# Decode scores in three runs a half batch, and the next chunk's first gate products ahead of a chunk's down products

## The chip, the cores and the metric

The kernel runs on one core of one Trainium2 chip. The metric is the device time of one execution in microseconds (us), from the first to the last instruction with what the device does around them. The kernel before takes 1250.42 us, the median of three runs (1248.77 to 1251.25).

The engines that the text speaks of: TensorE (PE in the profile, with its weight loads as PEld), VectorE (DVE), ScalarE (ACT), GpSimd (POOL), and SyncE (SP), which only issues DMAs here. Each runs its own list of instructions in order and waits for the others by semaphores.

## The reference, cut to what matters

One layer of a hybrid decoder is computed for a prompt group (512 tokens) and a sample group (8 sequences of 4 tokens, each with 4096 past tokens in a paged cache), with shared weights:

```python
h = h + 0.5 * rmsnorm(swiglu(rmsnorm(h, norm_g[0]), wg[0], wu[0], wd[0]), norm_g[1])
m, c_kv, k_r, s_fin = mixer(rmsnorm(h, norm_g[2]), ...)
h = h + rmsnorm(m, norm_g[3])
h = h + 0.5 * rmsnorm(swiglu(rmsnorm(h, norm_g[4]), wg[1], wu[1], wd[1]), norm_g[5])

def swiglu(x, wg, wu, wd):
    return (jax.nn.silu(x @ wg) * (x @ wu)) @ wd
```

Inside the mixer, the sample group attends to its cache in latent form. For each of the 8 sequences, 16 queries (4 tokens by 4 heads) of 256 + 64 elements meet 4096 past rows:

```python
s = (einsum('bqhr,bsr->bhqs', ql, c_kv) + einsum('bqhd,bsd->bhqs', qr, k_rope)) * scale
p = softmax(s)
out = einsum('bhqs,bsr->bqhr', p, c_kv)
```

## The kernel before

All big products are made of three fp32r matmuls for each pair of operands: a value is split in a high part (`wh`, `uh`, `hh`) and a remainder (`wl`, `ul`, `hl`). `weight` (lines 230 to 251) loads a weight block into `wraw` by an SP DMA, casts it to `wh` on ACT (line 250) and makes `wl` on DVE (line 251). The tokens are handled in two parts, `a` (256 columns) and `b` (288).

The change lies in one stage. There the second feed-forward network runs for part `a`, and woven into it is the decode attention of the sample group.

**The feed-forward side** is the generator `ffn(..., fine=True)`, called `gb`. It goes over 22 blocks `f` of the hidden width, in four chunks of 6, 6, 5 and 5 blocks (`FCH`). For a block it computes a gate product (24 matmuls: 8 blocks of depth by 3) and an up product (24), both at line 277, then `silu(gate) * up`, which is split into `hha` and `hla`. At the end of a chunk come the down products of the chunk for 8 column blocks `d`: the first two together in `gemm_2` (line 288), the others in `gemm` (line 259). They need the `hha` and `hla` of all the chunk's blocks. With `fine`, a gate or up product yields after half of it, so that a step of `gb` is 12 matmuls, or one down product.

**The decode side** is the generator `decode`, called `ga`. A half batch `H[n]` is 2048 past rows of one sequence; there are 16. Its work is spread over several rounds `n` of five steps `st`:

- POOL gathers two blocks of latent rows (`craw`, 1 MB each, line 1352, into seven slots) and two of rotary rows (`rraw`, line 1359, two buffers).
- DVE transposes them in five turns (`turn`, line 1367; two transposes each) into `kh`, a ring of four buffers (`KHB = 4`). `JS` says which columns a turn takes: the rotary rows first. `rraw` is free once the first turn has read it, and `gather_r` fetches the next.
- PE makes the scores in five parts (`score(k)`, line 1379). A part is 16 fp32 matmuls on tiles of 64 by 32 of the array, which the trace shows as 32 records. All parts add into two PSUM tiles `s`, copied out after the last one by ACT and DVE (line 1385). `RUNS` says at which step which parts are issued: before, parts 0 to 2 at step 2 and parts 3 and 4 at step 4.
- One round later, at step 1 (`PEAK`), `peak` finds the maximum (`pm`, line 1391), takes the exponentials (line 1397), transposes them and copies them to `pbuf` (line 1403, 12 copies on ACT and 4 on DVE); at step 4, `value` multiplies with `craw` (line 1412, 32 records).

A loop calls `ga` 94 times and `gb` 100 times by turns. A scheduler then orders each engine's list by readiness and priority, within the dependences; what it made is read from the built program's list.

The names of the steps: **run** is a row of score matmuls with no other PE work between them. **round** is the five steps.

Of the kernel before, what the change touches and what calls it, by code (L numbers as in the profile page):

```python
# [14 lines left out]
ALU = mybir.AluOpType  # L15
AX = mybir.AxisListType

P = 128
D = 1024
KD = D // P  # L20
# [5 lines left out]
HS = (256, T - 256)  # L26
# [38 lines left out]
JS = ((8, 9), (0, 1), (2, 3), (4, 5), (6, 7))  # L65
KHB = 4
PEAK = 1
RUNS = {2: (0, 1, 2), 4: (3, 4)}
LEVELS = (32, 16, 8, 4, 2, 1)
CH = 64  # L70

# [39 lines left out]
def hybrid_step_kernel(  # L111
# [5 lines left out]
    nc = tc.nc  # L117
# [55 lines left out]
    def tmp(tag, n, bufs=2, pool=sb):  # L173
        return mk([P, HM], F32, tag, bufs, pool=pool)[:, :n]
# [57 lines left out]
    def weight(srcs, kt, staged=False, home=None):  # L232
        if home is None and staged:
            pool, sfx, bufs = st, "x", STAG
        elif wx and wcnt[0] % (NW + WX) >= NW:
            pool, sfx, bufs = wx[0], "", WX
        else:
            pool, sfx, bufs = sb, "", NW
        w = mk([P, 8, P], F32, "wraw", 5, pool=sb)
        if home is None:  # L240
            wh = mk([P, 8, P], F32R, "wh" + sfx, bufs, pool=pool)
            wl = mk([P, 8, P], F32R, "wl" + sfx, bufs, pool=pool)
            wcnt[0] += not staged
        else:
            wh, wl = home
        n = P // len(srcs)
        for i, s in enumerate(srcs):
            nc.sync.dma_start(w[:, :kt, i * n : (i + 1) * n], s)
        with tc.issue_after(behind[1].ins) if behind[1] is not None else nullcontext():
            nc.scalar.copy(wh[:, :kt], w[:, :kt])  # L250
        nc.vector.tensor_tensor(wl[:, :kt], w[:, :kt], f32(wh[:, :kt]), op=ALU.subtract)  # L251
        return wh, wl, kt
# [16 lines left out]
    def gemm_q(wt, act_, step=2):  # L269
        wh, wl, kt = wt  # L270
        acc = ps("acc", "acc")
        n = act_[0].shape[-1]
        for k in range(kt):
            if k and k % step == 0:
                yield
            for i, (a, b) in enumerate(((wh, act_[0]), (wh, act_[1]), (wl, act_[0]))):
                nc.tensor.matmul(acc[:, :n], a[:, k], b[:, k], start=k + i == 0, stop=k == kt - 1 and i == 2)  # L277
        return acc[:, :n]
# [14 lines left out]
    def wcols(w, k0, kt, c0):  # L293
        return w[c0 // P, :, k0 : k0 + kt]
# [29 lines left out]
    def ffn(i, n_post, xs, u, nxt=None, mid=None, late=None, fin=None, pre=(), fine=False):  # L324
        pool = cur[-1]
        yield
        r2 = {x: u[x][2] for x in xs}
        mT = {x: actslot("m", x) for x in xs}
        ends = []
        for c, (f0, nf) in enumerate(FCH[i]):  # L330
            hh = {x: mk([P, FCH[i][0][1], HS[x]], F32R, "hh" + "ab"[x], pool=pool) for x in xs}
            hl = {x: mk([P, FCH[i][0][1], HS[x]], F32R, "hl" + "ab"[x], pool=pool) for x in xs}
            for j in range(nf):
                f = f0 + j
                wg_ = (w0 or [weight([wcols(w_g[i], 0, KD, f * P)], KD)]).pop(0)
                ga, up = {}, {}
                for x in xs:
                    ga[x] = (yield from gemm_q(wg_, u[x], 4)) if fine else gemm(wg_, u[x])
                if fine:
                    yield  # L340
                if late and f == 0:
                    behind[0] = late()
                wu_ = (w0 or [weight([wcols(w_u[i], 0, KD, f * P)], KD)]).pop(0)
                for x in xs:
                    up[x] = (yield from gemm_q(wu_, u[x], 4)) if fine else gemm(wu_, u[x])
                behind[1] = behind[0] if f == 1 else None
                for x in xs:
                    s = tmp("sil", HS[x], 3, pool)
                    t = tmp("sit", HS[x], 2, pool)
                    nc.vector.tensor_tensor(s, ga[x], r2[x], op=ALU.mult)  # L350
                    sigmoid(t, s)
                    nc.vector.tensor_tensor(s, s, t, op=ALU.mult)
                    nc.vector.tensor_tensor(s, s, up[x], op=ALU.mult)
                    split(hh[x][:, j], hl[x][:, j], s)
                yield
            last = c == len(FCH[i]) - 1
            if fin and c == BEG:
                fin.begin(u[xs[0]][2])
            if last:
                sacc = {x: tmp("ssm" + "ab"[x], HS[x], 1, pool) for x in xs}  # L360
            groups = [(d,) for d in range(KD)] if not last or len(xs) == 1 else [(d,) for d in range(KD - STAG)] + [tuple(range(KD - STAG, KD))]
            for grp in groups:
                if fine and not last and grp[0] == 0:
                    accs = yield from gemm_2([weight([wcols(w_d[i], f0, nf, d * P)], nf) for d in (0, 1)], (hh[xs[0]], hl[xs[0]]))
                elif fine and not last and grp[0] == 1:
                    accs = accs[1:]
                else:
                    accs = None
                wts = None if accs else {d: pre.pop(0) if pre else weight([wcols(w_d[i], f0, nf, d * P)], nf, len(grp) > 1) for d in grp}
                for x in xs:  # L370
                    for d in grp:
                        acc = accs[0] if accs else gemm(wts[d], (hh[x], hl[x]))
                        if last and fin and d == KD - 1:
                            fin.sums(sacc[x])
                        if c == 0:
                            nc.scalar.copy(mT[x][:, d], acc)
                        else:
                            nc.vector.tensor_tensor(mT[x][:, d], mT[x][:, d], acc, op=ALU.add)
                        if last:
                            sq = scale_sq(sacc[x], mT[x], d, gq, n_post, bool(fin) and d == KD - 1)  # L380
                        if last and fin and LAG <= d:
                            fin.column(mT[x], d - LAG)
                    if last and grp is groups[-1] and fin:
                        with tc.issue_after(fin.scale(sq).ins):
                            for d in range(KD - LAG, KD):
                                fin.column(mT[x], d)
                        fin.end(mT[x])
                    elif last and grp is groups[-1]:
                        ends.append(post(x, mT[x], sacc[x], u[x][2], nxt))
                        next(ends[-1])  # L390
                if not accs or grp[0] == 0:
                    yield
        if mid:
            mid()
        for p in ends:
            for _ in p:
                pass
# [14 lines left out]
    w0 = []  # L412
# [875 lines left out]
    with scope("dec"):  # L1288
# [134 lines left out]
        def decode():  # L1423
            H = [Half(n) for n in range(NH2)]
            blocks = [h_ for h_ in H for _ in range(2)]
            ups = [(h_, st) for h_ in H for st in range(len(JS))]

            def gather(n=1):
                for h_ in blocks[:n]:
                    h_.gather()  # L1430
                del blocks[:n]

            def turn():
                if ups:
                    h_, st = ups.pop(0)
                    h_.turn(st)
                    if st == 0 and h_.n + 1 < NH2:
                        H[h_.n + 1].gather_r()

            for n in range(NH2 + 4):  # L1440

                def at(k):
                    return H[n - k] if 0 <= n - k < NH2 else None

                for st in range(len(JS)):
                    if at(2):
                        for k in RUNS.get(st, ()):
                            at(2).score(k)
                    if n < 3 and st == 0:
                        if n == 0:  # L1450
                            H[0].gather_r()
                        gather(2 + n // 2)
                    if st == PEAK and at(3):
                        at(3).peak()
                    if st == 1 and at(4) and at(4).i:
                        at(4).gathered()
                    if st == len(JS) - 1 and at(3):
                        for c in range(2):
                            at(3).value(at(4), c)
                            gather()  # L1460
                    if n > 1 or n == 1 and st >= 1:
                        if n != 2 or st >= 2:
                            turn()
                    yield

        def decode_end():
# [228 lines left out]
```

## Time and profile before

| what | us |
|---|---|
| median of three runs | 1250.42 |
| the profiled execution, its own time | 1257.12 |
| its span from first to last instruction | 1255.3 |
| PE busy in it | 1225.7 |
| DVE busy in it | 983.8 |
| ACT busy in it | 742.0 |
| first and last score matmul, from the span's start | 716.2 and 953.2 |

The granted TensorE clock is 0.995 over the span and 1.00 from 716 us to 980 us.

A row of the timeline is: start, duration, engine, line, operation, output and inputs, the tile of the array, the shape, the number of equal instructions merged, and in brackets the idle time before it with what ended it. Matmuls overlap, so the durations of merged rows count from the first start to the last modelled end; the pitch, from start to start, is what PE spends. A row of waits is: who waited, for whom, in total, how often, the longest. A row of windows has for PE, PEld, DVE, ACT and POOL the busy time and the instructions, then the clock, the DMA share and the GB/s.

### The profile page before, as it was taken

The page shows a single profiled execution, that of the slowest core. Times are in us where ns is not written, and L with a number is a line of the kernel's source. Part 1 is how long each engine was busy: PE and PEld are TensorE (multiplying, and loading weights), DVE is VectorE, ACT ScalarE, POOL GpSimd, SP SyncE. Part 2 cuts the span into 40 slices and gives each one's busy share as a digit, 9 for nine tenths or more (in the row PEclk, how much of TensorE's full clock was granted, in tenths as well). Part 3 has the DMA queues.
Part 4 walks back from the last instruction along what each step waited for, and adds up shares of the span by engine and source line. Part 5 has one row for each costly group of instructions (what it writes and reads, how often), then busy time and mean ns, then how long its engine had stood idle before and what let it go on. Part 6 is the DMA issues. An engine that isn't in the chain of part 4 may idle for free.

```text
span 1255.3 us, 30001 instructions
## 1 busy us (share of the span) xinstructions
PE 1225.7 (98%) x12366; PEld 1157.1 (92%) x12366; DVE 983.8 (78%) x1976; ACT 742.0 (59%) x1559; POOL 72.4 (6%) x80
## 2 busy tenths in 40 slices
PE   8999999999999999999999899999999999999997
PEld 7999999999999988988889889878888999999997
DVE  7897788878679887877876899989987878466665
ACT  7675545544466655446668656665656777554454
POOL 0000000000000000000000412222310000000000
PEclk9999999999999999999999899999999999999999
DMA  6232333322164122324223959778776635645551
GB/s 236 85 118 87 100 101 101 94 96 94 51 227 158 60 89 69 104 77 148 75 92 118 374 178 347 292 249 299 252 273 218 204 104 191 188 137 182 145 160 59
DMA packets 73113, 195.59 MB, mean 156 GB/s; under 512 B 12336, under 2 KB 27728, under 8 KB 68240
## 3 DMA queue, kind: packets, MB, share of 16 engines
q1 hardware_dynamic: 64512, 150.47, 37.0%
q0 software_dynamic: 7168, 41.95, 9.2%
q8 instruction: 97, 1.59, 0.5%
q10 hardware_dynamic: 1296, 1.26, 0.3%
q14 instruction: 40, 0.33, 0.1%
HBM read 183.97 MB, written 9.67 MB: 154 GB/s over the span
## 4 chain that ended last, share of the span: by engine, by line
PE 86%; ACT 6%; DVE 5%; issue 2%; DMA 1%; SPq 0%; DVEq 0%; ACTq 0%
PE acc L259 29%; PE acc L277 18%; PE dn L259 8%; PE Y L561 6%; PE X L561 4%; PE Z L561 4%; PE s L1379 3%; PE acc L717 3%; PE o L1412 2%; ACT wh L250 1%; DVE wl L251 1%; PE pa L938 1%; ACT pbuf L1403 1%; PE acc L288 1%; PE zx L826 1%
## 5 line engine op out<-in xcount | busy, mean ns | idle before, releaser
L250 ACT CAST wh<-wraw 128x1024 fp32r<-128x1024 f32 (+2 forms) x194 | 185.3, 959 | 169.3 <-PE acc L259 108.6
L251 DVE TENSOR_TENSOR wl<-wraw,wh 128x1024 fp32r<-128x1024 f32 (+2 forms) x194 | 214.3, 1107 | 68.6 <-ACT wh L250 67.5
L277 PE MATMUL acc<-uha,wh 128*128 128x256 f32 (+1 forms) x528 | 155.7, 296 | 0.8 <-ACT uha L207 0.8
L277 PE MATMUL acc<-uha,wl 128*128 128x256 f32 (+1 forms) x528 | 150.6, 286 | 0.5 <-DVE wl L251 0.4
L277 PE MATMUL acc<-ula,wh 128*128 128x256 f32 (+1 forms) x528 | 150.9, 286 | 0.0
L259 PE MATMUL acc<-uhb,wh 128*128 128x288 f32 (+1 forms) x432 | 128.0, 296 | 0.0
L259 PE MATMUL acc<-uhb,wl 128*128 128x288 f32 (+1 forms) x432 | 127.0, 295 | 0.9 <-DVE wl L251 0.7
L259 PE MATMUL acc<-ulb,wh 128*128 128x288 f32 (+1 forms) x432 | 127.5, 295 | 0.0
L277 PEld LDWEIGHTS acc<-uha,wh 128*128 128x128 f32 x528 | 99.6, 189 | 8.8 <-issue 7.3
L277 PEld LDWEIGHTS acc<-uha,wl 128*128 128x128 f32 x528 | 99.5, 189 | 2.4 <-DVE wl L251 1.4
L277 PEld LDWEIGHTS acc<-ula,wh 128*128 128x128 f32 x528 | 99.8, 189 | 1.5 <-issue 1.2
L259 PEld LDWEIGHTS acc<-uhb,wl 128*128 128x128 f32 x432 | 81.2, 188 | 1.5 <-DVE wl L251 1.5
L259 PEld LDWEIGHTS acc<-uhb,wh 128*128 128x128 f32 x432 | 81.0, 188 | 0.2 <-ACT uhb L170 0.2
L259 PEld LDWEIGHTS acc<-ulb,wh 128*128 128x128 f32 x432 | 81.1, 188 | 0.1
L259 PE MATMUL dn<-hh,dh 128*128 128x272 f32 x256 | 74.3, 290 | 0.0
L259 PE MATMUL dn<-hh,dl 128*128 128x272 f32 x256 | 73.8, 288 | 0.0
L259 PE MATMUL dn<-hl,dh 128*128 128x272 f32 x256 | 73.6, 287 | 0.0
L1379 PE MATMUL s<-kh,q 64*32 64x128 f32 x2560 | 53.5, 273 | 5.3 <-issue 5.3
L277 PE MATMUL acc<-uhb,wh 128*128 128x272 f32 x176 | 52.8, 300 | 0.0
L1379 PEld LDWEIGHTS s<-kh,q 64*32 64x32 f32 x2560 | 38.5, 105 | 15.4 <-issue 10.5
L259 PE MATMUL acc<-hlb,wh 128*128 128x288 f32 x176 | 52.1, 298 | 0.0
L259 PE MATMUL acc<-hhb,wh 128*128 128x288 f32 x176 | 51.8, 298 | 0.0
(632 smaller groups left out, 3899.0 us busy)
## 6 DMA issues: line engine op xcount, KB each, us to landing
wraw<-w_u SPq DMA_DIRECT2D x66, 512.0 KB
wraw<-w_g SPq DMA_DIRECT2D x65, 512.0 KB
wraw<-w_d SPq DMA_DIRECT2D x40, 384.0 KB
wraw<-w_in SPq DMA_DIRECT2D x24, 512.0 KB
wraw<-w_d SPq DMA_DIRECT2D x32, 320.0 KB
wraw<-w_d SPq DMA_DIRECT2D x16, 512.0 KB
wraw<-w_o SPq DMA_DIRECT2D x16, 512.0 KB
g_S<-state SPq DMA_DIRECT2D x4, 512.0 KB
```

The source lines that it names most:

```text
L250: nc.scalar.copy(wh[:, :kt], w[:, :kt])
L251: nc.vector.tensor_tensor(wl[:, :kt], w[:, :kt], f32(wh[:, :kt]), op=ALU.subtract)
L259: nc.tensor.matmul(out, a, b, start=n == 0, stop=n == last)
L277: nc.tensor.matmul(acc[:, :n], a[:, k], b[:, k], start=k + i == 0, stop=k == kt - 1 and i == 2)
L288: nc.tensor.matmul(acc, a[:, k], b[:, k], start=k + i == 0, stop=k == kt - 1 and i == 2)
L561: nc.tensor.matmul(bank, a[p][:, k], b[q][:, k], start=first and k + n == 0, stop=k == 3 and n == 2, skip_group_check=True)
L717: nc.tensor.matmul(accs[x, d], wts[d][p][:, k], hs[k // 2][q][:, k % 2, x], start=k + n == 0, stop=k == nf - 1 and n == 2)
L826: nc.tensor.matmul(z, w[a][:, k], U[1][b][:, k], start=k + n == 0, stop=k == KD - 1 and n == 2)
L938: nc.tensor.matmul(po[es, c].rearrange("p (n m) -> p n m", m=m), kx[:, cs], up(qx[:, cs], m), start=True, stop=True, skip_group_check=True)
L1379: nc.tensor.matmul(self.s[r][c * 32 : c * 32 + 32, :P], q[rs, j], kh, start=st + jj == 0, stop=st == len(JS) - 1 and jj == 1, skip_group_c ...
L1403: (nc.scalar.copy if g else nc.vector.tensor_copy)(self.p[g * 32 : g * 32 + 32, c // 2, c % 2 * 4 : c % 2 * 4 + 4, self.i * 16 : self.i * ...
L1412: nc.tensor.matmul(o[g : g + 32, :R], self.p[:, c, a], self.craw[c][:, a], start=i + c == 0 and a < 4, stop=i + c == 2 and a >= 4, skip_gr ...
```

## The change

`RUNS` now gives the parts in three runs: 0 and 1 at step 0, 2 and 3 at step 2, 4 at step 4. So the first parts come two steps earlier, and the transposes that feed them do too: the exception for round 2 is dropped, and all later turns of `kh` stand two steps ahead of their old place.

In `ffn`, the gate product of a block and the `silu` behind it are taken out into `gate` and `swish`. With `fine`, at the end of a chunk that isn't the last, the gate product of the next chunk's first block is issued ahead of the chunk's down products, and its `silu` right behind it.

```diff
-RUNS = {2: (0, 1, 2), 4: (3, 4)}
+RUNS = {0: (0, 1), 2: (2, 3), 4: (4,)}
...
+        def swish(x, z):
+            s = tmp("sil", HS[x], 3, pool)
+            t = tmp("sit", HS[x], 2, pool)
+            nc.vector.tensor_tensor(s, z, r2[x], op=ALU.mult)
+            sigmoid(t, s)
+            nc.vector.tensor_tensor(s, s, t, op=ALU.mult)
+            return s
+
+        def gate(f):
+            w = (w0 or [weight([wcols(w_g[i], 0, KD, f * P)], KD)]).pop(0)
+            z = {}
+            for x in xs:
+                z[x] = (yield from gemm_q(w, u[x], 4)) if fine else gemm(w, u[x])
+            if fine:
+                yield
+            if late and f == 0:
+                behind[0] = late()
+            return {x: swish(x, z[x]) for x in xs} if fine else z
+
+        ahead = None
...
-                wg_ = (w0 or [weight([wcols(w_g[i], 0, KD, f * P)], KD)]).pop(0)
-                ga, up = {}, {}
-                for x in xs:
-                    ga[x] = (yield from gemm_q(wg_, u[x], 4)) if fine else gemm(wg_, u[x])
...
+                up = {}
+                sg = ahead if ahead else (yield from gate(f))
+                ahead = None
...
-                    s = tmp("sil", HS[x], 3, pool)
-                    t = tmp("sit", HS[x], 2, pool)
-                    nc.vector.tensor_tensor(s, ga[x], r2[x], op=ALU.mult)
-                    sigmoid(t, s)
-                    nc.vector.tensor_tensor(s, s, t, op=ALU.mult)
+                    s = sg[x] if fine else swish(x, sg[x])
                     nc.vector.tensor_tensor(s, s, up[x], op=ALU.mult)
                     split(hh[x][:, j], hl[x][:, j], s)
                 yield
             last = c == len(FCH[i]) - 1
+            if fine and not last:
+                ahead = yield from gate(f0 + nf)
...
-                        if n != 2 or st >= 2:
-                            turn()
+                        turn()
```

Each engine has the same instructions as before, by kind and shape; only their order differs, from the start of the decode stage to its end. What follows shows the list where the prediction looks at it.

PE, in one round in the middle of the stage, before (`pm` is the maximum of one half batch, `s` the scores of the next, `o` first the copied products of a finished pair turned around, then the products with the gathered slots `uhb` and `ha`; "..." stands for the network's matmuls):

```order
L1391 MATMUL pm<-ident,mxh 128x128
L1420 MATMUL o<-q_8159,q_8787 128x32 x2
...
L1379 MATMUL s<-kh,q_8159 32x128 x48
...
L1379 MATMUL s<-kh,q_8159 32x128 x32
L1412 MATMUL o<-uhb,pbuf 32x256 x8
L1412 MATMUL o<-ha,pbuf 32x256 x8
```

and the same round now:

```order
L1393 MATMUL s<-kh,q_8159 32x128 x32
...
L1405 MATMUL pm<-ident,mxh 128x128
L1434 MATMUL o<-q_8159,q_8787 128x32 x2
...
L1393 MATMUL s<-kh,q_8159 32x128 x32
...
L1393 MATMUL s<-kh,q_8159 32x128 x16
L1426 MATMUL o<-uhb,pbuf 32x256 x8
L1426 MATMUL o<-ha,pbuf 32x256 x8
```

There is one run more in a round, the first stands ahead of `pm`, and after the products with the slots only 12 of the network's matmuls stand ahead of the next round's first run. Over the whole list there are 37 runs before and 52 now; the rounds of the first two half batches are cut into more pieces in both.

DVE in the same round, before, from the transpose of the exponentials on (`hb`, `mb`, `q`, `dx` are gathered slots, `hla` and `sil` belong to the network):

```order
L1399 STREAM_TRANSPOSE pt<-q_8159 128x256
L1403 COPY pbuf<-pt 32x4x16 x4
L1367 STREAM_TRANSPOSE kh<-hb 128x512
L1367 STREAM_TRANSPOSE kh<-mb 128x512
L1367 STREAM_TRANSPOSE kh<-rraw 128x512 x2
L171 TENSOR_TENSOR hla<-sil,hha 128x256
L1367 STREAM_TRANSPOSE kh<-q_8787 128x512
L1367 STREAM_TRANSPOSE kh<-dx 128x512
```

and now:

```order
L1381 STREAM_TRANSPOSE kh<-hb 128x512
L1381 STREAM_TRANSPOSE kh<-mb 128x512
L336 TENSOR_TENSOR sil<-sil,sit 128x256
L1381 STREAM_TRANSPOSE kh<-rraw 128x512
L1407 TENSOR_REDUCE q_8159<-pm 128x16
L1435 COPY q_8787<-o 128x4x16
L1410 SCALAR_TENSOR_TENSOR mq,mbd<-q_8159 128x16
L1381 STREAM_TRANSPOSE kh<-rraw 128x512
L1413 STREAM_TRANSPOSE pt<-q_8159 128x256
L365 TENSOR_TENSOR sil<-sil,acc 128x256
L1417 COPY pbuf<-pt 32x4x16 x4
```

The turn of the rotary rows stood behind the copies to `pbuf`; now it stands ahead of them, in this round around the maximum `pm`.

SP, at the end of the network's first chunk, before and then now (`w_g`, `w_u` and `w_d` are the weights of gate, up and down products):

```order
L248 DMA wraw<-w_u 128x1024
L248 DMA wraw<-w_d 128x768 x8
L248 DMA wraw<-w_g 128x1024
L248 DMA wraw<-w_u 128x1024
```

```order
L248 DMA wraw<-w_u 128x1024
L248 DMA wraw<-w_g 128x1024
L248 DMA wraw<-w_d 128x768 x8
L248 DMA wraw<-w_u 128x1024
```

One gate weight of 512 KB went ahead of eight down weights, at each of the three boundaries between chunks, and its products with it.

More of the change, by code (lines that the diff above doesn't have):

```diff
@@ L334, in ffn @@
                 f = f0 + j
-                wg_ = (w0 or [weight([wcols(w_g[i], 0, KD, f * P)], KD)]).pop(0)
-                ga, up = {}, {}
-                for x in xs:
-                    ga[x] = (yield from gemm_q(wg_, u[x], 4)) if fine else gemm(wg_, u[x])
[L339 to L342, printed above, removed]
+                up = {}
+                sg = ahead if ahead else (yield from gate(f))
+                ahead = None
                 wu_ = (w0 or [weight([wcols(w_u[i], 0, KD, f * P)], KD)]).pop(0)
```

## The prediction

> **What bounds the kernel now.** I read the page's head first, then the stage that changes by windows, then who waits there, then the timeline of single rounds.
>
> ```profile
> span 1255.3 us, 30001 instructions
> PE 1225.7 (98%) x12366; PEld 1157.1 (92%) x12366; DVE 983.8 (78%) x1976; ACT 742.0 (59%) x1559; POOL 72.4 (6%) x80
> ```
>
> PE is the bound over the whole span. The lists of the two kernels differ in the decode stage alone, so only what PE spends there can change. This is the row of the stretch in which the rounds are regular, thirteen half batches from 752.75 to 947.78 us:
>
> ```profile
> 752.75:947.78 195.03, 189.07 (x3499) 163.16 (x3498) 177.00 (x390) 118.58 (x314) 46.38 (x47) 1.00 0.80 283
> ```
>
> PE is busy for 189.07 of 195.03 us, but DVE for 177.00, with the same work after the change. However much PE gains there, the stretch can't fall below 177: DVE is a second bound 18 us away. The waits of PE and of its weight loads from 716 to 955 us:
>
> ```profile
> PE s L1379 <- issue: 5.3, 18, 0.4
> PE acc L288 <- ACT hha L170: 0.6, 1, 0.6
> PE acc L277 <- DVE wl L251: 0.4, 1, 0.4
> PE pm L1391 <- DVE mxh L1387: 0.4, 1, 0.4
> ```
>
> ```profile
> PEld s L1379 <- issue: 10.5, 20, 0.6
> ```
>
> PE hardly waits for another engine. What it does lose is inside the score runs, for "issue", which is nothing that the profile shows: 10.5 us by the weight loads, whose ends are short (PE's own row counts less, since the modelled ends of 0.27 us cover part of each gap). Here is the timeline of PE in one such run, then that of GpSimd around it and after:
>
> ```profile
> 802.53 0.89 PE L1379 MATMUL s<-kh,q 64*32 64x128 f32 x42
> 803.59 0.43 PE L1379 MATMUL s<-kh,q 64*32 64x128 f32 x4 [0.17 <-issue]
> 804.34 0.42 PE L1379 MATMUL s<-kh,q 64*32 64x128 f32 x4 [0.32 <-issue]
> 805.06 0.51 PE L1379 MATMUL s<-kh,q 64*32 64x128 f32 x14 [0.29 <-issue]
> 805.49 0.42 PE L1412 MATMUL o<-uhb,pbuf 128*32 128x256 f32 x4
> ```
>
> ```profile
> 802.30 0.95 POOL L1359 DMA_INDIRECT rraw<-pool_r,idx  x1 [7.28 <-DVE kh L1367]
> 803.55 0.95 POOL L1359 DMA_INDIRECT rraw<-pool_r,idx  x1 [0.30 <-issue]
> 806.87 1.37 POOL L1352 DMA_INDIRECT uhb<-pool_c,idx  x1 [2.36 <-PE o L1412]
> 808.54 0.94 POOL L1352 DMA_INDIRECT ha<-pool_c,idx  x1 [0.30 <-issue]
> 816.57 0.95 POOL L1359 DMA_INDIRECT rraw<-pool_r,idx  x1 [7.09 <-DVE kh L1367]
> ```
>
> And a run of as many records that loses nothing, with GpSimd ahead of it:
>
> ```profile
> 774.92 1.16 PE L1379 MATMUL s<-kh,q 64*32 64x128 f32 x64
> 776.01 0.42 PE L1412 MATMUL o<-mb,pbuf 128*32 128x256 f32 x4
> ```
>
> ```profile
> 772.28 0.95 POOL L1359 DMA_INDIRECT rraw<-pool_r,idx  x1 [7.12 <-DVE kh L1367]
> 773.53 0.95 POOL L1359 DMA_INDIRECT rraw<-pool_r,idx  x1 [0.30 <-issue]
> ```
>
> The first takes 2.96 us to the next work (805.49 - 802.53), the second 1.09: 1.87 us are lost. In the first, after 42 records PE gets four at a time, at 0.04, 0.79 and 1.51 us after the second gather's start; in the second, the gathers began 2.6 us earlier and nothing happens. My reading, which is a coincidence of times and no more: while GpSimd issues two gathers, until 1.5 us after the second begins, PE's supply of instructions thins, and only a dense run (64 records in 0.9 us, against a network matmul each 0.12 us) empties what it has in store.
>
> **The change part by part.**
>
> *More runs.* A switch into and out of the score tiles:
>
> ```profile
> 811.71 0.28 PE L277 MATMUL acc<-ula,wh 128*128 128x256 f32 x1
> 811.83 0.28 PE L277 MATMUL acc<-uha,wl 128*128 128x256 f32 x1
> 812.03 1.59 PE L1379 MATMUL s<-kh,q 64*32 64x128 f32 x96
> 813.56 0.39 PE L277 MATMUL acc<-uha,wh 128*128 128x256 f32 x1
> ```
>
> The network's pitch is 0.12 (811.83 - 811.71), the step into the run 0.20, the pitch inside it (1.59 - 0.27) / 95 = 0.014, so its last record starts at 813.35 and the step out is 0.21. One run more costs 0.20 + 0.21 - 0.12 - 0.01 = 0.28 us, and 52 - 37 = 15 runs cost **+4.2**. Nothing hides it: PE is the bound. The Trainium skill, TensorEngine Tiling (Array Packing), section Key Properties, states that a change of the tiling mode drains the array; a drain of the last matmul's whole 0.28 us each way would make it 15 x 0.43 = 6.5 us, an estimate, and the measured 0.20 decides here.
>
> *The gate product ahead.* At a chunk's end the down products wait for the last `hla`:
>
> ```profile
> 847.03 0.38 PE L288 MATMUL acc<-hha,wh 128*128 128x256 f32 x1 [0.61 <-ACT hha L170]
> 847.49 0.39 PE L288 MATMUL acc<-hla,wh 128*128 128x256 f32 x1
> 847.71 0.28 PE L288 MATMUL acc<-hha,wl 128*128 128x256 f32 x1
> ```
>
> The gap ahead of 847.03 is 0.61 + 0.28 of the modelled end, the one behind it 0.46; less two pitches that is **-1.1**. Of the three boundaries only this one waits (the row of waits has it once). The 24 matmuls that now stand between, 2.8 us, cover it. The `silu` behind the gate product comes no earlier inside a chunk: the scheduler had already put it beside the up product. The gate weight's DMA passes eight down weights on SP, which then come 512 KB later and are wanted 24 matmuls later: 0, between -0.4 and +0.4, which is the one wait for `wl` that PE has in the stage.
>
> *The stalls in the runs.* Before, the run that is hit is the second, because the first turn of `kh`, which frees `rraw`, is done in between. It still is:
>
> ```profile
> 815.63 1.26 DVE L1367 STREAM_TRANSPOSE kh<-rraw 128x512 f32<-128x512 f32 x2
> ```
>
> ```profile
> 816.60 0.67 PE L1379 MATMUL s<-kh,q 64*32 64x128 f32 x32
> ```
>
> Here the gather (816.57) began 4.54 us after the first run (812.03) and the second run 4.57. Now the second run begins 0.9 + 0.2 + 1.3 + 0.25 + 1.3 + 0.2, or 4.1 us after the first (4.5 with the extra products `o`). On DVE, `rraw` waits for part 1 and stands behind a pair (1.3) and a `silu` product (0.4): part 0 ends at 0.7, so the gather can begin at 0.7 + 1.3 + 0.4 + 0.7 + 0.3 = 3.4, later by as much as DVE is behind, which is up to 1 us. So it meets the second run again, of 64 records as before. Bounds: all 10.5 us gone, if DVE is so late that the run is over; or 1.87 in each of 14 runs, 26, which is 15.7 more. I take **0**, the pattern as it is.
>
> *A run closer to the latent gathers.* These begin when the products `o` free a slot (806.87 and 808.54 above), and the next run was 6.5 us away (805.49 to 812.03); now only 12 matmuls stand between.
>
> ```profile
> 807.36 0.39 PE L277 MATMUL acc<-uha,wh 128*128 128x256 f32 x1
> ```
>
> The run would begin at 807.36 + 1.3 + 0.2 = 808.9, have its 42 records by 809.5 and, if these gathers act as the others do, stall until 808.54 + 1.5 = 810.0: 0.5 us, 7 in 14 rounds. No row shows a run there. Between 0 and 7 I take **+1**: PE's products in between use little.
>
> *New and moved waits.* The first run now reuses the score tiles 3.4 us after the products `o` begin (808.9 - 805.49), and waits for both copies of the last scores.
>
> ```profile
> 790.34 0.42 PE L1412 MATMUL o<-dx,pbuf 128*32 128x256 f32 x4
> ```
>
> ```profile
> 794.40 0.25 DVE L1385 COPY q<-s 128x128 f32<-128x128 f32 x1
> ...
> 807.96 0.25 DVE L1385 COPY q<-s 128x128 f32<-128x128 f32 x1
> ```
>
> By the first pair the copy ends 4.3 us behind `o` (0.9 late), by the second 808.21 - 805.49 = 2.7 (in time). Behind the waiting run stand only PE's own products, and DVE's turn for part 0. Between 0 and 14 x 0.9 = 13 I take **+0.5**. The wait of `pm` for the maximum (0.4) goes, since a run and 1.4 us more stand ahead of `pm`: **-0.5**. From `pm` to `o` there stood the first run, 24 matmuls and the second run; now there are 12 matmuls (1.6 with the edges), then run, 24 matmuls and run (0.9 + 0.2 + 2.7 + 0.2 + 0.4 + 0.2 = 4.6): 6.2 us, and 1.2 more until the last quarter of `o`.
>
> ```profile
> 810.30 0.38 PE L1391 MATMUL pm<-ident,mxh 128*128 128x128 f32 x2
> ```
>
> ```profile
> 813.77 3.09 ACT L1403 COPY pbuf<-pt 32x64 f32<-32x64 f32 x12 [1.16 <-DVE pt L1399]
> ```
>
> The copies to `pbuf` end 6.6 us after `pm` (816.86), the last quarter wants them at 7.4: 0, with 0.8 us in hand, and up to 5 if ACT and DVE are later in a third of the rounds. The turns of `kh` come two steps closer to their gathers; DVE waits for none of these now, and the slot `uhb`, issued at 806.87, is read at 817.41. That reserve shrinks by some 3 us: 0, at most 3 a round.
>
> ```profile
> 817.41 0.67 DVE L1367 STREAM_TRANSPOSE kh<-uhb 128x512 f32<-128x512 f32 x1
> ```
>
> **Sum:** 4.2 - 1.1 + 0 + 1 + 0.5 - 0.5 = **+4.1 us**. On the profiled execution's own 1257.12 this is 1261.2. That one lies 6.7 us above the median of the runs shown, so I carry the difference over: 1250.42 + 4.1 = **1254.5**.
>
> **The rivals.**
>
> The row of PE's instruction queue, which the first rival's page speaks of:
>
> ```profile
> q8 instruction: 97, 1.59, 0.5%
> ```
>
> *Faster: the runs come clear of the gathers.* If DVE lags enough that the rotary gathers begin behind the second run, the 10.5 us go, and the third run of 32 records is too short to be hit. That gives 4.2 - 1.1 - 10.5 + 0.5 - 0.5 = -7.4, or **1243**. For it speaks that DVE is busy for 91% of the stretch and its list between two first runs is no shorter; against it, that the two distances (3.4 and 4.1) leave only 0.7 us, as they were 4.54 and 4.57. It decides when the gather is 0.6 us later than the run's start. The Trainium skill, Runtime: NRT & Kernel Launch, section Instruction fetch mechanics, states that instructions are refilled in blocks of 16 KiB ahead of use and that crossing a block is mostly hidden. The trace agrees on the blocks (1.59 MB in 97 packets is 16.4 KB each), not on the hiding: by that rule a run would owe nothing to a late supply and this rival would be void, which the 42 records and the fours behind them speak against.
>
> *Same: DVE sets the pace.* If the stalls only give DVE the time that it needs anyway, then the new cost falls into its slack: **1250.4**, within 2.5. For it: 177.00 of 195.03 busy. Against it: PE's rows show few waits for DVE.
>
> *Slower by more: both kinds of gather hit,* the second run as at 802 in most rounds (+5) and the first by 0.5 (+6 beyond the 1): **1265**.
>
> **How the numbers follow.** Forecast (1254.5, its own range 1253 to 1259) 0.42; faster 0.28; same 0.20; slower by more 0.10. About 0.2%, or 2.5 us, is what a measurement of this kernel can tell from no change; the low edge of the forecast's range gives 0.04 to "same". Faster 0.28, same 0.24, slower 0.48. The range of 1243 to 1262 takes in the rival of the stalls and the unknown waits, and leaves out most of the case of both gathers.
>
> **What would show it.** Runs of 32, 32 and 16 matmuls with 0.20 us at each edge, 15 more of them; no gap ahead of line 288; the row "s <- issue" near 10 us for the weight loads. It falls if that row shrinks or doubles, if PE gets rows of waits for the copies of the scores or for `pbuf`, or if DVE waits for the gathered slots.

## The result, and the profile after

| | median us | runs | from, to |
|---|---|---|---|
| before, beside the changed kernel | 1249.57 | 7 | 1248.53, 1251.25 |
| the changed kernel | 1253.46 | 7 | 1252.40, 1255.01 |

The changed kernel takes 1.0022 times the time of before, 95% interval [1.0013, 1.0032]: 2.8 us slower by the ratio, 3.9 by the medians. A second comparison (third group below) gives 1.0025 [1.0015, 1.0034]. The prediction was 1254.5.

The head of the profile after, and the windows' row of its regular stretch (columns as before):

```profile
span 1251.0 us, 30033 instructions
PE 1224.7 (98%) x12366; PEld 1154.5 (92%) x12366; DVE 983.3 (79%) x1976; ACT 738.9 (59%) x1559; POOL 77.9 (6%) x80
```

```profile
752.00:944.00 192.00, 190.09 (x3515) 162.01 (x3522) 177.22 (x393) 117.06 (x318) 52.08 (x47) 1.00 0.80 284
```

The profiled execution's own time is 1252.79, near its median. That of before was 1257.12, above every timed run of it. Set side by side, the two traces would make the changed kernel 4 us faster; the timed runs say the opposite. So the first thing to settle is the profile of before.

The waits of PE and of its weight loads from 716 to 955 us in the profile after:

```profile
PE s L1393 <- issue: 0.9, 2, 0.5
PE acc L277 <- DVE wl L251: 0.8, 2, 0.5
PE o L1426 <- ACT pbuf L1417: 0.4, 1, 0.4
PE s L1393 <- ACT q L1399: 0.2, 1, 0.2
```

```profile
PEld o L1426 <- ACT pbuf L1417: 3.1, 7, 0.6
...
PEld s L1393 <- issue: 1.3, 2, 0.8
PEld s L1393 <- DVE q L1399: 0.6, 2, 0.4
```

The 10.5 us of "s <- issue" have shrunk to 1.3, the wait ahead of the down products is gone, and the wait for `pbuf` has grown. Before, its row was:

```profile
PEld o L1412 <- ACT pbuf L1403: 1.4, 3, 0.6
```

Here is its timeline after, with an undisturbed run of the same 16 records from a later round:

```profile
757.53 1.36 PE L1426 MATMUL o<-ha,pbuf 128*32 128x256 f32 x16 [0.36 <-ACT pbuf L1417]
759.02 1.41 PE L1426 MATMUL o<-hb,pbuf 128*32 128x256 f32 x16
...
847.08 1.05 PE L1426 MATMUL o<-uhb,pbuf 128*32 128x256 f32 x16
848.06 0.39 PE L288 MATMUL acc<-hha,wh 128*128 128x256 f32 x1
```

By the starts of the trace's records, the step into these products takes 0.63 us there instead of 0.20, and their 32 records 2.52 instead of 1.55. That is 1.4 us; one later round loses 0.5 more. The last row is the chunk's end at 848: the first down product follows without a gap.

### The profile page after: what moved, and what is told of

Read it like the earlier page. It is cut to its first block, busy times and chain, and to the rows that moved or that the text cites. A ratio compares the mean times of both kernels' runs of the same rounds, so it can differ in the third digit from the quotient of the medians.

```text
span 1251.0 us, 30033 instructions
## 1 busy us (share of the span) xinstructions
PE 1224.7 (98%) x12366; PEld 1154.5 (92%) x12366; DVE 983.3 (79%) x1976; ACT 738.9 (59%) x1559; POOL 77.9 (6%) x80
## 3 DMA queue, kind: packets, MB, share of 16 engines
q8 instruction: 97, 1.59, 0.5%
## 4 chain that ended last, share of the span: by engine, by line
PE 84%; DVE 7%; ACT 6%; issue 1%; DMA 1%; SPq 0%; DVEq 0%; ACTq 0%
PE acc L259 30%; PE acc L277 16%; PE dn L259 8%; PE Y L575 7%; PE X L575 4%; PE Z L575 4%; PE acc L731 3%; PE s L1393 3%; PE o L1426 2%; DVE kh L1381 2%; DVE wl L251 1%; ACT wh L250 1%; PE acc L288 1%; PE pa L952 1%; ACT pbuf L1417 1%
## 5 line engine op out<-in xcount | busy, mean ns | idle before, releaser
L259 PE MATMUL acc<-hhb,wl 128*128 128x288 f32 x176 | 51.5, 295 | 0.0
```

The costliest lines, as they stand in the source:

```text
L259: nc.tensor.matmul(out, a, b, start=n == 0, stop=n == last)
```

## The experiments

Each kernel was run beside before on the same chip. There were three groups of four, on three chips. Before took 1250.6 us (29 runs) on the first, 1257.8 (21 runs) on the second, 1251.0 (32 runs) on the third. The second is slower for the same program; times are compared across chips by the ratio to before alone.

I use one number beside the time: the **loss inside the runs**, worked out from the starts of PE's records from 745 us on. A run of 96 records takes 1.32 us from first to last start when nothing holds it, one of 64 takes 0.89, one of 32 takes 0.40; what is over that, summed over all runs, is the loss. It counts every delay inside a run, also a wait for another engine.

### First group: before, its halves, and two runs at the early place

`e1_before` has no edit.

> The kernel before, unchanged, profiled once more. Its first profile was of an execution of 1257.1 us, its timed runs are at 1249.6. Theory A (a run's two edges are the price; the stalls inside the score runs belong to the one long execution): this profile's own time is near 1249.6, and the weight loads of the score runs lose under 3 us to issue. Rival B (the stalls are in every execution of before, and the changed kernel lost 10 us elsewhere that its trace does not show): 8 to 12 us of issue again, with a span near 1248.

Measured: ratio 0.9999 [0.9991, 1.0008]; the profiled execution's own time is 1251.32. Its waits of PE from 716 to 955 us, the run that lost 1.87 us in the prediction's trace, and GpSimd beside it:

```profile
PE pm L1391 <- DVE mxh L1387: 3.9, 6, 1.1
PE acc L288 <- ACT hha L170: 1.1, 1, 1.1
PE acc L288 <- DVE hla L171: 0.7, 1, 0.7
PE acc L277 <- DVE wl L251: 0.4, 1, 0.4
```

```profile
802.22 1.16 PE L1379 MATMUL s<-kh,q 64*32 64x128 f32 x64
803.30 0.42 PE L1412 MATMUL o<-uhb,pbuf 128*32 128x256 f32 x4
```

```profile
801.95 0.95 POOL L1359 DMA_INDIRECT rraw<-pool_r,idx  x1 [7.28 <-DVE kh L1367]
803.21 0.95 POOL L1359 DMA_INDIRECT rraw<-pool_r,idx  x1 [0.30 <-issue]
```

Theory A holds, B falls. The same program, with the gathers 0.27 us ahead of the run and 0.99 behind its start (0.23 and 1.02 in the prediction's trace), loses nothing: 0.1 us over all runs against 11.6. The row "s <- issue" isn't among the waits. So the stalls of the prediction's profile are no part of the 1250 us. In their place PE waits for DVE ahead of the maximum `pm` and, at two chunks' ends, ahead of the down products:

```profile
757.68 0.39 PE L288 MATMUL acc<-hla,wh 128*128 128x256 f32 x1 [0.67 <-DVE hla L171]
...
845.09 0.39 PE L288 MATMUL acc<-hha,wh 128*128 128x256 f32 x1 [1.08 <-ACT hha L170]
845.55 0.39 PE L288 MATMUL acc<-hla,wh 128*128 128x256 f32 x1
```

By starts, with the modelled end of 0.28 and the pitch of 0.12 as in the prediction: 0.67 + 0.28 - 0.12 = 0.83; 1.08 + 0.28 - 0.12 = 1.24; 0.46 - 0.12 = 0.34. In all 2.4 us that the gate product ahead can take away, not 1.1. The stalls had hidden such waits: from first to last score matmul the prediction's trace is 6.0 us longer than this one (237.1 and 231.1). Its runs lose 11.5 us more inside, but `pm` waits 4.6 less and the chunks' ends 1.3 less, all by starts, which leaves 5.6.

`e2_runs` is the changed kernel without the gate product ahead:

```diff
-            if fine and not last:
-                ahead = yield from gate(f0 + nf)
```

> The three runs a half batch alone, without the gate product ahead (52 runs of scores, before has 37). Theory A: 15 runs x 0.28 = +4.2 us on before, and the gap of 1.1 at the chunk's end stays: 1254 to 1255, some 1 us above the changed kernel, and the gap of about 0.6 us ahead of the two down products is in its profile. Rival C (the gate product ahead is what costs, by its weight's DMA or its silu): 1249 to 1250.

Measured: 1254.9 us, ratio 1.0036 [1.0023, 1.0049], so 4.5 above before. The wait ahead of the down products is there (1.3 us). C falls: the three early runs carry the whole loss.

`e3_gate` is the other half:

```diff
-RUNS = {0: (0, 1), 2: (2, 3), 4: (4,)}
+RUNS = {2: (0, 1, 2), 4: (3, 4)}
...
-                        turn()
+                        if n != 2 or st >= 2:
+                            turn()
```

> The gate product ahead alone, the runs of scores as before (37). Theory A: -1.1 on before, 1248.5, with no gap ahead of the two down products. Rival C: 1253 to 1254, like the changed kernel.

Measured: 1248.36 us, ratio 0.9981 [0.9973, 0.9990], 2.2 below before by the medians and 2.4 by the ratio. That is twice what A had written, and what the rows of `e1_before` give. Other waits moved too: in its rows PE waits 2.5 us for `pm` (3.9 in `e1_before`) and 0.9 for the turns of `kh` (none there).

`e4_two` has two runs a half batch at the changed kernel's places:

```diff
-RUNS = {0: (0, 1), 2: (2, 3), 4: (4,)}
+RUNS = {0: (0, 1), 2: (2, 3, 4)}
```

> The changed kernel with two runs a half batch: parts 0 and 1 at step 0, parts 2 to 4 at step 2 (37 runs, as before), the turns and the gate product as changed. It takes away the 15 extra runs and leaves the first one where the change put it. Theory A: 4.2 us below the changed kernel, 1249.3, give or take 0.7. Rival D (it is the early place that costs: the first run behind the copies of the last scores and near the gathers, and the products with the slots that come sooner behind pm): 1252.5 to 1254.

Measured: 1254.0 us, ratio 1.0027 [1.0016, 1.0037]. With 15 runs fewer it is no faster than the changed kernel. By the number A fails and D comes true, but the trace shows a cause that neither had named: the loss inside the runs is 7.1 us, all in the second run of a round, now 96 records long. Its largest:

```profile
912.38 1.11 PE L1393 MATMUL s<-kh,q 64*32 64x128 f32 x57
914.85 0.86 PE L1393 MATMUL s<-kh,q 64*32 64x128 f32 x39 [1.36 <-issue]
```

TensorE's instructions are loaded in blocks of 16 KB (97 packets with 1.59 MB in the table of DMA queues). This trace has 24917 records of PE and PEld, semaphore instructions counted in: 257 to a packet, and 256 is what I count by. Counted in records from the start, all six gaps over 0.3 us of this kernel stand at the same part of a block, and all of them end 1.29 to 1.48 us after the landing of the block that was under way. Worked out from the trace's records and its DMA packets:

```
kernel      gap (us)            records/256   block's load      landing to end of gap
e4_two      752.47 to 753.86    51.75         751.62 to 752.57  1.29
e4_two      913.22 to 914.85    74.76         912.13 to 913.40  1.45
changed     888.00 to 888.76    70.76         886.40 to 887.37  1.39
changed     901.39 to 902.04    72.75         899.73 to 900.69  1.35
```

My reading is that TensorE has come to the end of what is loaded. In all four rows the first late record is number 193 of its 256. In none of the traces does a record of that number start less than 1.2 us after the landing of its block, taking the blocks in order. The last two rows show that the changed kernel meets it too. Here is the first of them in its timeline:

```profile
887.15 1.12 PE L1393 MATMUL s<-kh,q 64*32 64x128 f32 x60
888.76 0.41 PE L1393 MATMUL s<-kh,q 64*32 64x128 f32 x4 [0.49 <-issue]
```

Four of the 64 records come 0.76 us late. In `e1_before` TensorE is never at the end: at the block that it reaches soonest after a landing, at 903.28 us, the landing lies 1.56 us back. Its runs are of 96 and 64 records too, and its shortest block is used up in 4.7 us (5.1 in `e4_two`), so length alone doesn't make a stop: the load has to land late as well.

### Second group: on the slower chip

`e6_three_late` splits the runs at the late places, with the gate product ahead; only the number of runs differs from `e3_gate`:

```diff
-RUNS = {2: (0, 1, 2), 4: (3, 4)}
+RUNS = {2: (0, 1), 3: (2,), 4: (3, 4)}
```

> The gate product ahead, with three runs a half batch at the old late places: parts 0 and 1 at step 2, part 2 at step 3, parts 3 and 4 at step 4 (52 runs), where the gate product alone with 37 runs took 1248.4 us. Only the number of runs differs. Theory A (0.28 us for each further run): 15 x 0.28 = +4.2, 1252.6. Theory D (the runs cost little, the early place costs): 1248.4 to 1249.5.

`e5_five` is the changed kernel with a run for each part:

```diff
-RUNS = {0: (0, 1), 2: (2, 3), 4: (4,)}
+RUNS = {0: (0,), 1: (1,), 2: (2,), 3: (3,), 4: (4,)}
```

> The changed kernel with one run for each part, five a half batch (81 runs, the changed kernel has 52). Theory A: 29 x 0.28 = +8.1 on 1253.5, so 1261.6, or 1258.7 if the 2.9 us that the changed kernel's score runs lost inside vanish with shorter runs. Theory D: 1253.5, since the first part stands where it did.

`e7_edge` moves the runs against the blocks:

```diff
             s = ps("s")
+            for _ in range(64):
+                nc.tensor.matmul(s[:, :TS], idb, newb, start=True, stop=True)
             for j in range(3):
```

> The kernel with two runs at the early places (1254.0 us), with 64 small matmuls on its sample group's scores of the new rows ahead of the decode stage, whose results nothing uses; by the pitch of small bf16 matmuls 2 to 5 us. They move the 16 KB blocks of TensorE's instructions by half a block against the runs. Theory E (TensorE stops at a block's edge until 1.3 to 1.5 us after the block's load has landed): each long gap inside a run stands where the count of TensorE's records has the part 0.25 of a block of 256, not 0.75 as before, and ends 1.3 to 1.5 us after a load's landing. Theory G (the gathers of GpSimd starve it): the gaps stay in the same rounds and at the same records, with the part 0.25 by chance alone.

`e8_peak` issues the maximum later:

```diff
-PEAK = 1
+PEAK = 2
...
+                    if st == PEAK and at(3):
+                        at(3).peak()
                     if at(2):
                         for k in RUNS.get(st, ()):
                             at(2).score(k)
...
-                    if st == PEAK and at(3):
-                        at(3).peak()
```

> The gate product ahead alone (1248.4 us, runs as before), with the maximum of a half batch issued one step later, ahead of the first run instead of 12 matmuls ahead of it. Its matmul waited for DVE for about 2.5 us by TensorE's rows and some 4 by those of its weight loads. If that wait is time of the kernel: 1245 to 1246.5, as long as the copies to pbuf, which now begin 1.4 us later, do not make the products with the slots wait; if they do (0.3 us in each of 16 rounds), 1248 to 1250.

Measured, where before took 1257.8 us:

| kernel | us | ratio to before, interval | loss inside the runs |
|---|---|---|---|
| three runs late | 1259.1 | 1.0011 [1.0002, 1.0021] | 9.8 |
| five runs | 1262.4 | 1.0034 [1.0021, 1.0047] | 4.1 |
| two runs early, moved | 1263.7 | 1.0047 [1.0035, 1.0060] | 15.3 |
| maximum later | 1261.6 | 1.0029 [1.0019, 1.0038] | 14.6 |

The expectations were in times of the first chip and can't be held against these. What can be read is the kind of stall. One run of `e8_peak`, and GpSimd beside it:

```profile
792.76 0.65 PE L1393 MATMUL s<-kh,q 64*32 64x128 f32 x27
793.82 0.44 PE L1393 MATMUL s<-kh,q 64*32 64x128 f32 x5 [0.41 <-issue]
794.58 0.42 PE L1393 MATMUL s<-kh,q 64*32 64x128 f32 x4 [0.32 <-issue]
795.29 0.50 PE L1393 MATMUL s<-kh,q 64*32 64x128 f32 x12 [0.29 <-issue]
```

```profile
792.52 0.95 POOL L1373 DMA_INDIRECT rraw<-pool_r,idx  x1 [11.11 <-DVE kh L1381]
793.78 0.95 POOL L1373 DMA_INDIRECT rraw<-pool_r,idx  x1 [0.30 <-DVE kh L1381]
```

This is the pattern of the prediction's profile: fours and fives, most of the gaps 0.56 to 0.60 us between starts, until 1.5 us after the second gather's start. Such gaps stand at any part of a block and end 0 to 10 us after a landing, so they aren't the stop at a block's end. The first profile of before, with 1257.12 us, fits this chip's 1257.8; that it was taken on such a chip is my reading, not shown. A run of 32 records loses little: `e5_five`, all of such runs, 4.1 us. Its 44 more runs than before would cost 12.3; less about 7.5 saved inside the runs (11.6 to 4.1) and 1.1 to 2.4 for the gate product that is 2.4 to 3.7, with 4.3 measured. The 11.6 are from that first profile of before, since none was taken on this chip, so the sum is an estimate. `e8_peak` settles nothing, for the gate product alone was not run on this chip.

### Third group: on a chip like the first

The same kernels as `e3_gate`, `e6_three_late` and `e7_edge`, and the changed kernel.

> The changed kernel, unchanged, beside the next three. The chip of the last four runs took 1257.8 us for the kernel before, those ahead of them 1250. Where before takes 1250: 1253.5 again, with under 4 us lost inside the score runs. Where it takes 1258, its own score runs lose 12.7 us, by its first profile. Theory G (the gathers starve a dense run there): the second run of 64 records of a round is met as often as before, and the changed kernel loses 10 to 13 too, 1260 to 1262. Theory H (shorter runs of 64 and 32 instead of 96 and 64 are mostly spared): under 6 us lost, 1254 to 1257, that is no slower than before.

> The gate product ahead alone, once more. 1.1 to 2.2 us below before on either chip: 1248.4 where before takes 1250.6, 1255.5 to 1256.7 where it takes 1257.8.

> The gate product ahead with three runs at the late places, once more, now beside the gate product alone on the same chip; only the number of runs differs, 52 for 37. Theory A (0.28 us a run, nothing hides it): 4.2 above it. Theory F (the wait of the maximum's matmul for DVE, about 4 us in the gate product's profile where before takes 1250, shrinks by what the runs add): 0 to 1.5 above it there, with that wait under 1 us in the profile.

> Two runs at the early places with 64 small matmuls ahead of the stage, once more. Where before takes 1250: by theory E the long gaps inside the runs stand at the part 0.25 of a block of 256 records, 0.75 in the same kernel without the small matmuls, each 1.3 to 1.5 us behind the landing of a block; by theory G they stand 0 to 2 us behind the start of a gather at any part of a block. Where before takes 1258: gaps of 0.56 to 0.60 us behind four to six records each, as in the first look, about 15 us in all, and theory E can't be told there.

Measured, where before took 1250.98 us:

| kernel | us | ratio to before, interval | loss inside the runs |
|---|---|---|---|
| changed | 1253.8 | 1.0025 [1.0015, 1.0034] | 4.0 |
| gate product ahead alone | 1248.06 | 0.9981 [0.9972, 0.9990] | 2.7 |
| with three runs late | 1251.8 | 1.0014 [1.0005, 1.0023] | 1.9 |
| two runs early, moved | 1251.83 | 1.0012 [1.0003, 1.0021] | 3.9 |

Before took 1251 us here, so what the expectations say of a chip with 1258 wasn't met: theories G and H of the changed kernel stay untested.

**The price of a run.** From the second row to the third only the number of runs differs, 37 and 52: 3.7 us by the medians, 4.1 by the ratios (1.0014 / 0.9981). Theory A said 4.2. The starts in the two traces say the same. The steps into and out of all score runs take 15.72 us in the first and 21.86 in the second; less the 15 network pitches and 15 run pitches that they replace (2.0), the 15 runs cost 4.1. Theory F falls: the wait for the maximum is 2.1 us in the first and 1.8 in the second. PE's waits, first for the gate product alone, then with three late runs:

```profile
PE pm L1405 <- DVE mxh L1401: 2.1, 2, 1.2
PE s L1393 <- DVE kh L1381: 1.1, 2, 0.9
```

```profile
PE pm L1405 <- DVE mxh L1401: 1.8, 2, 0.9
PE s L1393 <- DVE kh L1381: 0.5, 2, 0.3
PE acc L277 <- DVE wl L251: 0.2, 1, 0.2
```

The long gaps inside the runs of these two kernels are mostly this wait for the turns of `kh`. With three late runs, for instance, one ends at 844.82 us, 0.06 us after a transpose.

**The early place.** From the third row to the first the runs are as many, but stand early: 2.0 us by the medians, 1.4 by the ratios. The loss inside the runs is 2.1 more, and three of the changed kernel's four gaps over 0.25 us in this trace stand at a block's end; the fourth is a wait for the copy of the last scores.

**The two chips.** `f3_three_late` is the program of `e6_three_late`. From first to last score it takes 232.0 us here and 240.1 there, and from there to the last matmul 294.8 and 294.7. The loss inside the runs is 1.9 and 9.8. `f4_edge` and `e7_edge` are one program too: 228.0 and 239.7, with 3.9 and 15.3. So in these two pairs the slower chip is slower by the stalls inside the runs and by nearly nothing else.

**The blocks.** The moved kernel has four gaps over 0.25 us where `e4_two` had six, in other rounds: 800, 814, 828 and 842 us, where that had 752, 769, 872, 886, 900 and 913. One of them:

```profile
812.72 1.55 PE L1395 MATMUL s<-kh,q 64*32 64x128 f32 x83
814.95 0.44 PE L1395 MATMUL s<-kh,q 64*32 64x128 f32 x13 [0.68 <-issue]
```

```
kernel      gap (us)            records/256   block's load      landing to end of gap
f4_edge     800.65 to 801.49    58.75         799.22 to 800.18  1.30
f4_edge     814.00 to 814.95    60.76         812.55 to 813.47  1.48
f4_edge     827.73 to 828.37    62.76         826.04 to 827.01  1.36
f4_edge     842.25 to 842.53    64.75         840.14 to 841.11  1.42
```

My expectation had the sides crossed. The count takes in the 128 new records, so a block's end keeps its part of 0.75, and what moves by half a block is the score matmul that stands there. Gaps that belong to certain records of the program would have come to 0.25. All four are at 0.75, so it is the block's end, and theory G falls for this kind of gap. The time agrees, if weakly: the kernel is 1.5 us above before by the ratio (0.85 by the medians) where `e4_two` was 3.4 above, with intervals that overlap, though the 64 matmuls take 1.6 us (698.0 to 699.6). With these, if nothing hid them, and the 3.9 us inside the runs taken off, it would be 1251.83 - 1.6 - 3.9 = 1246.3; the gate product alone, without its own 2.7, would be 1245.4. By this sum the early place costs near 1 us beside the loss inside the runs; it is an estimate, since 2.0 of the 2.7 are waits for the turns of `kh`.

## Why the prediction came out as it did

*The sum.* +4.1 was forecast; 2.8 and 3.9 (ratio and medians of the first comparison), 3.1 and 2.8 (those of the third chip) were measured. The time lies in the forecast's own range, but not every term does.

*More runs, +4.2: right, and shown.* 3.7 to 4.1 for the same 15 runs at the late places. The measured edges of 0.20 and 0.21 us hold; a drain of the whole last matmul each way (6.5) does not.

*The gate product ahead, -1.1: right in its mechanism, half its size.* -2.2 and -2.9 were measured by the medians of two chips, -2.4 by both ratios. The forecast took the one gap of a profile in which PE had lost 10 us to stalls. Without the stalls two chunk ends wait, 2.4 us by starts. That the stalls gave ACT and DVE time to get ahead fits the two traces of before, but no run here took the stalls alone away. This is the term that was mis-sized.

*The stalls, 0: the right number for a wrong reason.* The step that failed is "the pattern as it is". On chips with 1250 us the pattern isn't there before, and not there after; what is there after is a loss of 2.9 to 4.0 us, some of it at blocks' ends (0.76 + 0.65 of 2.9 in the first trace). By the prediction's own signs it falls: the row "s <- issue" shrank from 10.5 to 1.3, and rows for the copies of the scores and for `pbuf` came. That the time is right is in part luck: these terms and the gate product's were off in opposite directions. The conjecture on GpSimd's gathers fits the slower chip, but gathers at the same distance cost nothing on the others, so they are not enough. The prediction also read the fours and fives as speaking against the hiding of loads at block ends. They don't stand at block ends; what speaks against it are the stops in the tables above.

*Carrying the difference to the median: right.* Taking 4.1 off 1250.42 and not off 1257.12 was what kept the number right, for the 6.7 us between go with stalls that the timed runs of before don't have (0.1 us in `e1_before`).

*Near the latent gathers +1, copies of scores +0.5, wait of `pm` -0.5, `pbuf` 0: the sum is near, the terms are not.* The early place measured 1.4 to 2.0, and the longer gaps stand at block ends, not where a latent gather was expected to stall a run. Between the traces of before (`e1_before`) and of the changed kernel on the third chip: the loss inside the runs +3.9; `pbuf` +1.4, where I had 0.8 us in hand; the copies of the last scores 0.6, once, at 821 us, of which 0.3 stands ahead of the run; the wait for `wl` +0.4; `pm` -5.3 by starts (3.9 in PE's rows of waits), where the forecast had the 0.4 of a disturbed trace. With the runs and the gate product that is 4.1 - 2.4 + 3.9 + 1.4 + 0.3 + 0.4 - 5.3 = 2.4, with 2.5 between these two executions' own times. Terms under 0.4 us are not in the sum, so part of this agreement is chance.

*The rivals.* "The runs come clear of the gathers" foresaw the row "s <- issue" as it came, at 1.3, and the time didn't follow, since before didn't have these stalls in its timed runs. "DVE sets the pace" was right in that before waits for DVE at `pm`, which the change took away, but what the runs cost fell into no slack.

*What stays open:* why one chip adds stalls near indirect gathers and others don't, and what delays a block's load (it starts between 1.7 us before and 5.1 us after TensorE has passed the end of the block before, in the changed kernel's first trace).

The version that beats both is the gate product ahead with the runs as they were: 1248.4 and 1248.1 us on two chips, 0.9981 of before each time. It wasn't set against before on the slower chip.

## What to carry to other kernels

Where a profiled execution lies outside the timed runs, profile the kernel again before pricing anything: stalls of one execution hide waits that are real in the others, and the sign of a comparison can come out wrong, as it did between the two first profiles here. On a bound TensorE each further switch between tile shapes costs its two edges in full, here 0.28 us, so short work of another shape belongs together. A long run can also use up the loaded instructions, as in `e4_two`; no length at which that begins was found, for `e1_before` has runs as long and no stop. And a product from the next chunk ahead of a chunk's end is cheap cover for the last element-wise work.

## What the runs showed of the hardware

Where TensorE stops at the end of a 16 KB block of instructions, it goes on 1.29 to 1.53 us after the next block has landed; it cost up to 1.63 us at once and most of the 7.1 us in `e4_two` (5.5 in its six gaps). Network products are met too: one waits 0.35 us at 770 us in the changed kernel's second trace. A block is 128 matmuls with their weight loads, 15 us of the network's (128 at 0.12); where two score runs fall into it, it is used up in 5.1 us (`e4_two`). Where the ends fall depends on every instruction ahead: 64 matmuls put in 16 us before the stage moved all the gaps. The Trainium skill, Runtime: NRT & Kernel Launch, Instruction fetch mechanics, states that crossing a block is mostly hidden. In `e1_before` it is; in the changed kernel, `e4_two` and `f4_edge` it is not, by the gaps above.

One program differed between chips by 7 us (1250.6 and 1257.8), and in the two programs that were profiled on both, the difference lies in this stage. About half of the gaps over 0.25 us in the score runs there are 0.56 to 0.60 us long.
